# Transposes of a decoder layer moved from TensorE to VectorE and the GpSimd queue

## The chip, the cores and the metric

The kernel runs on one core of a Trainium2 chip. It is one program: one launch computes a whole decoder layer. The metric is the device time of one execution in microseconds (us).

## What is computed

One decoder layer on 256 tokens of width 2048 in float32, with a final RMS norm. The reference, cut to its skeleton:

```python
def parallel_mixer(h, w_in, ..., cos, sin, lam_init):
    z = h @ w_in
    qa, ka, va, qb, kb, vb, ga, gb = split_columns(z, IN_WIDTHS)
    qa, ka = partial_rope(qa, cos, sin), partial_rope(ka, cos, sin)
    oa = differential_attention(qa, ka, va, lam)      # 8 heads, two softmax maps each
    oa = rms_norm(oa, da_subln_g) * (1.0 - lam_init)  # per head, 128 values
    ob = stick_breaking_attention(qb, kb, vb)         # 8 heads, strictly causal
    merged = sigmoid(ga) * (oa @ w_proj_a) + sigmoid(gb) * (ob @ w_proj_b)
    return merged @ w_out

def reference(x, mem, ...):
    x = x + parallel_mixer(rms_norm(x, norm_mix_g), ...)
    x = x + memory_cross_attention(rms_norm(x, norm_x_g), rms_norm(mem, norm_mem_g), ...)
    x = x + conv_ffn(rms_norm(x, norm_ffn_g), ...)    # gated, causal convolution of width 3
    return rms_norm(x, final_norm_g)
```

## The kernel before

All weights stream from HBM in pieces of 1 MB, which the SyncE queue loads. `product` (L193) multiplies them: every piece is cut into two tiles of two 128-row blocks; ACT casts a tile to its high part (`whi`, L179), VectorE forms the low part (L180), and TensorE computes three matmuls for each block and token tile (high by high, high by low, low by high: L185 to L187). A tile costs TensorE 12 matmuls of 512 columns, a unit of 2048 rows by 512 columns costs 96. There are three buffers each for high and low parts, so a cast waits until the matmuls of the tile three before it are done. Sums stand in four PSUM buffers `mm`; a unit takes two, one for each half of the tokens, so a unit can start only when the sums of the unit two before it have been evicted.

The units run in this order: mixer queries, keys and values qa0, ka0, va0, qa1, ka1, va1 (differential attention) and qb0 to vb1 (stick-breaking), eight gates g12 to g19, four merge units (pa and pb, 8 blocks each, for n = 0 to 3), the output projection wo0 to wo3 with the first residual, then cross keys kx, queries qx and values vx, the cross output wxo, the up-projections and the down-projections.

Between the matmuls stands the other work. `product` calls `tick` after each tile; `spawn(generator, delay)` puts a piece of work on a list, and `tick` runs due pieces up to their next `yield`. That sets the order in which the code is written out. A scheduler then orders the instructions of each engine anew by its own timing model when the program is compiled, all but SyncE's; each engine executes its row in that fixed order.

An operand of a matmul needs its contraction axis on the partitions, so results have to be transposed:

- `proj_T` (L260) evicts a unit of queries or keys from PSUM by ACT (L266, scaled by the norm factor, into a buffer of the pool `wk`), rotates it on GpSimd where needed, and two ticks later transposes it by 8 TensorE transposes of 128 x 128 (L275) through PSUM and copies it out on VectorE (L277).
- `transposed` (L142) does the same in two halves (L151) and splits each into a high and a low part by ACT and VectorE (`split`, L117 and L118, or L122 and L123 with gains). Merge units (`mT`), both residuals (`x1T`, `x2T`) and the cross queries and keys (`proj_T2`, L251) use it.
- `turn` and `regroup` (L129, L138), which only the up-projection uses: VectorE transposes 32 x 32 blocks within a tile, and 16 transfers of 32 KB issued by GpSimd put the blocks into their places.

The pool `wk` has seven buffers of one kind (`w2`). They hold the evicted queries and keys before their transposition, and also the score maps, exponentials and outputs of the attention heads. A differential head (`diff_head`) is a chain: scores on TensorE (`sa`), mask, maxima, exponentials, scaling and combination on VectorE and ACT (`pa`), three transposes (`da_tp`), the product with the values (`oa`), a norm over 128 values whose power -0.5 GpSimd takes (L351), two transposes (`oaT`) and a split. Heads 0 to 3 are spawned after va0, heads 4 to 7 after va1. A stick-breaking pair (`sb`, `lb`, `cb`, `ab`, `ob`) is the like with scans. In the views, numbers of buffers are left out, so `qaT_z` is an evicted unit of queries.

Of the kernel before, what the change touches and what calls it, by code (L numbers as in the profile page):

```python
# [11 lines left out]
AF = mybir.ActivationFunctionType  # L12
ALU = mybir.AluOpType
# [3 lines left out]
P = 128  # L17
S = 256
# [27 lines left out]
def hybrid_layer(ctx: ExitStack, tc: tile.TileContext, x, xT, mem, memT, gmix, par, gfin,  # L46
# [16 lines left out]
    def col(name, i=None, n=1):  # L63
        if name == "g_mix":
            return gm[:, i:i + n]
        a, b = _PC[name]
        return pc[:, a:b] if i is None else pc[:, a + i:a + i + n]
# [21 lines left out]
    def spawn(gen, delay=0):  # L89
        tasks.append([clock[0] + delay, gen])  # L90
# [16 lines left out]
    def chunk_tile(name, shape):  # L107
        return b4.tile(shape, F32, tag="b4", name=name)

    def sm_tile(name):  # L110
        return ps_sm.tile([P, U], F32, tag="sm", name=name)
# [15 lines left out]
    def turn(blk, src, t):  # L127

        nc.vector.transpose(out=blk[:, :, t * P:(t + 1) * P], in_=src.rearrange("p (f c) -> p f c", c=P))  # L129
# [11 lines left out]
    def flip_tile(name):  # L141
        return chunk_tile(f"{name}_blk", [P, U // P, S])  # L142

    def transposed(dst, src, n, name, gains=None):

        for h in range(2):
            pt = sm_tile(f"{name}_tp").rearrange("p (j s) -> p j s", j=2)
            for j in range(2):
                for t in range(NT):
                    c = (2 * h + j) * P  # L150
                    nc.tensor.transpose(out=pt[:, j, t * P:(t + 1) * P],  # L151
                                        in_=src[:, t, c:c + P], identity=ident)
            k0 = 4 * n + 2 * h
            dst[k0 // 2] = act_tile(f"{name}_{h}")
            split(dst[k0 // 2], pt, None if gains is None else [gains(k0), gains(k0 + 1)])
        yield 0

    def sumsq(dst, src):
        junk = wk.tile([P, U], F32, tag="w2", name="junk")
        nc.scalar.activation(out=junk[:, :src.shape[-1]], in_=src, func=AF.Square, accum_out=dst)  # L160
# [87 lines left out]
                                op=ALU.mult)  # L248
        nc.gpsimd.tensor_tensor(out=v[:, :, 0:ROT], in0=a, in1=b, op=ALU.add)

    def proj_T2(ps, r, name):  # L251

        dst = [None, None]
        z = chunk_tile(f"{name}_z", [P, NT, U])
        for t in range(NT):
            nc.scalar.activation(out=z[:, t], in_=ps[t], func=AF.Copy, scale=r[:, t:t + 1])
        spawn(transposed(dst, z, 0, name), 2)
        return dst

    def proj_T(ps, r, name, rotate=False):  # L260

        dst = chunk_tile(name, [P, 4, S])
        zs = []
        for t in range(NT):
            z = wk.tile([P, U], F32, tag="w2", name=f"{name}_z")
            nc.scalar.activation(out=z, in_=ps[t], func=AF.Copy, scale=r[:, t:t + 1])  # L266
            if rotate:
                rope(z, t)
            zs.append(z)

        def rest():
            for t in range(NT):
                pt = sm_tile(f"{name}_tp")
                for h in range(4):
                    nc.tensor.transpose(out=pt[:, h * P:(h + 1) * P],  # L275
                                        in_=zs[t][:, h * P:(h + 1) * P], identity=ident)
                nc.vector.tensor_copy(out=dst[:, :, t * P:(t + 1) * P],  # L277
                                      in_=pt.rearrange("p (h s) -> p h s", h=4))
            yield 0
        spawn(rest(), 2)  # L280
        return dst

    def proj_n(ps, r, name):
# [20 lines left out]
    def diff_head(h):  # L304
# [43 lines left out]
        nc.vector.tensor_scalar(out=tot, in0=ss[:, :, 0], scalar1=1.0 / P, scalar2=EPS,  # L348
                                op0=ALU.mult, op1=ALU.add)
        ro = st.tile([P, NT], F32, tag="ro", name="ro")  # L350
        nc.gpsimd.tensor_tensor(out=ro, in0=tot, in1=mhalf[:, :NT], op=ALU.pow)  # L351
        o = wk.tile([P, NT, P], F32, tag="w2", name="o")
        for t in range(NT):
            nc.vector.tensor_scalar(out=o[:, t], in0=po[:, t], scalar1=ro[:, t:t + 1], scalar2=None,
# [120 lines left out]
    for n in range(4):  # L475
        ga, gb = gates[n], gates[4 + n]
        for g in (ga, gb):
            nc.scalar.activation(out=g, in_=g, func=AF.Sigmoid)
        pa = product(oaT, w_pa, n, 8, f"pa{n}")
        pb = product(obT, w_pb, n, 8, f"pb{n}")  # L480
        for t in range(NT):
            nc.vector.tensor_tensor(out=ga[:, t], in0=pa[t], in1=ga[:, t], op=ALU.mult)
            nc.vector.tensor_tensor(out=gb[:, t], in0=pb[t], in1=gb[:, t], op=ALU.mult)
            nc.gpsimd.tensor_tensor(out=ga[:, t], in0=ga[:, t], in1=gb[:, t], op=ALU.add)
        spawn(transposed(mT, ga, n, f"mT{n}"), 2)

    def residual(ps, base, n, ss):
        for t in range(NT):
# [18 lines left out]
    for n in range(4):  # L507
        xr.append(chunk_tile(f"xr{n}", [P, NT, U]))
        nc.sync.dma_start(out=xr[n], in_=x[n])
        ps = product(mT, w_out, n, KD, f"wo{n}")  # L510
        residual(ps, xr[n], n, ss1)
        spawn(transposed(x1T, xr[n], n, f"x1T{n}", lambda k: col("g_x", k)), 2)
        if n == 0:
            spawn(load_mem(), 0)
    r1 = scaled(rstd(ss1, NT, D, "r1"), 128 ** -0.5, "r1x")


    rm = rstd(rmss, NT, D, "rm")
    kx = proj_T2(product(memTt, w_xkv, 0, KD, "kx"), rm, "kxT")
    qx = proj_T2(product(x1T, w_xq, 0, KD, "qx"), r1, "qxT")  # L520
    oxT = [act_tile(f"oxT{i}") for i in range(2)]
    pT = [None] * 4

# [204 lines left out]
```

## Time and profile before

| | us |
|---|---|
| median of 3 runs (1500.5 to 1500.92) | 1500.87 |
| the profiled execution | 1501.38 |
| its span in the trace | 1499.6 |
| TensorE busy, share of the span | 1484.7, 99% |
| VectorE, ACT, GpSimd busy | 919.5, 781.6, 256.2 |

The profile is of one execution. Its lines are grouped by source line, engine and operation; "idle before" names what an engine waited for last. Matmuls overlap, and their ends are modelled, so prices of TensorE work are read from starts.

### The profile page before, as it was taken

The page shows a single profiled execution, that of the slowest core. Times are in us where ns is not written, and L with a number is a line of the kernel's source. Part 1 is how long each engine was busy: PE and PEld are TensorE (multiplying, and loading weights), DVE is VectorE, ACT ScalarE, POOL GpSimd, SP SyncE. Part 2 cuts the span into 40 slices and gives each one's busy share as a digit, 9 for nine tenths or more (in the row PEclk, how much of TensorE's full clock was granted, in tenths as well). Part 3 has the DMA queues.
Part 4 walks back from the last instruction along what each step waited for, and adds up shares of the span by engine and source line. Part 5 has one row for each costly group of instructions (what it writes and reads, how often), then busy time and mean ns, then how long its engine had stood idle before and what let it go on. Part 6 is the DMA issues. An engine that isn't in the chain of part 4 may idle for free.

```text
span 1499.6 us, 17849 instructions
## 1 busy us (share of the span) xinstructions
PE 1484.7 (99%) x6728; PEld 1225.4 (82%) x6728; DVE 919.5 (61%) x1175; ACT 781.6 (52%) x1074; POOL 256.2 (17%) x424
## 2 busy tenths in 40 slices
PE   8999999999999999999999999999999999999997
PEld 6878788888888888888888888888888888888886
DVE  5566666565444555665676677767777776644562
ACT  6454455456444444664565555556655655444441
POOL 0202000000000010000003344334434433000010
PEclk9999999999999999999999999999999999999999
DMA  9544444545555556765445666666676666655561
GB/s 346 188 150 169 160 149 169 171 168 194 191 189 189 189 201 212 274 233 177 166 163 194 228 218 219 218 220 225 197 234 217 216 208 223 221 197 196 199 231 75
DMA packets 55270, 299.35 MB, mean 200 GB/s; under 512 B 10640, under 2 KB 10640, under 8 KB 22416
## 3 DMA queue, kind: packets, MB, share of 16 engines
q1 hardware_dynamic: 43488, 286.13, 54.8%
q0 software_dynamic: 11264, 11.56, 3.0%
q8 instruction: 52, 0.85, 0.2%
q10 hardware_dynamic: 432, 0.53, 0.1%
q14 instruction: 34, 0.28, 0.1%
HBM read 284.54 MB, written 2.10 MB: 191 GB/s over the span
## 4 chain that ended last, share of the span: by engine, by line
PE 98%; issue 1%; DMA 1%; DVE 0%; ACT 0%; SPq 0%; POOLq 0%; POOL 0%; DVEq 0%
PE up_mm L185 11%; PE up_mm L187 11%; PE up_mm L186 11%; PE dn_mm L186 5%; PE dn_mm L187 5%; PE dn_mm L185 5%; PE g_mm L185 4%; PE g_mm L187 4%; PE g_mm L186 4%; PE wo_mm L187 2%; PE wo_mm L186 2%; PE wo_mm L185 2%; PE va_mm L186 1%; PE qb_mm L186 1%; PE qb_mm L185 1%; PE kb_mm L187 1%
## 5 line engine op out<-in xcount | busy, mean ns | idle before, releaser
L180 DVE TENSOR_TENSOR up_lo<-up_raw,up_hi 128x1024 fp32r<-128x1024 f32 x176 | 214.5, 1223 | 130.7 <-ACT up_hi L179 130.7
L179 ACT CAST up_hi<-up_raw 128x1024 fp32r<-128x1024 f32 x176 | 184.9, 1050 | 192.2 <-PE up_mm L187 176.0
L187 PE MATMUL up_mm<-up_hi,x2T 128*128 128x512 f32 x704 | 273.9, 389 | 0.0
L186 PE MATMUL up_mm<-up_lo,x2T 128*128 128x512 f32 x704 | 273.9, 389 | 0.0
L138 POOL DMA_DIRECT2D uT<-up_blk x352 | 202.5, 583 | 287.8 <-DVE up_blk L129 169.1
L185 PE MATMUL up_mm<-up_hi,x2T 128*128 128x512 f32 x704 | 246.1, 389 | 0.0
L180 DVE TENSOR_TENSOR dn_lo<-dn_raw,dn_hi 128x1024 fp32r<-128x1024 f32 x88 | 109.8, 1253 | 94.9 <-ACT dn_hi L179 89.8
L187 PEld LDWEIGHTS up_mm<-up_hi,x2T 128*128 128x128 f32 x704 | 132.1, 188 | 27.5
L185 PEld LDWEIGHTS up_mm<-up_hi,x2T 128*128 128x128 f32 x704 | 132.2, 188 | 27.3
L186 PEld LDWEIGHTS up_mm<-up_lo,x2T 128*128 128x128 f32 x704 | 132.1, 188 | 27.4
L179 ACT CAST dn_hi<-dn_raw 128x1024 fp32r<-128x1024 f32 x88 | 91.8, 1054 | 115.2 <-PE dn_mm L187 99.9
L186 PE MATMUL dn_mm<-dn_lo,gT 128*128 128x512 f32 x352 | 136.9, 389 | 0.0
L187 PE MATMUL dn_mm<-dn_hi,gT 128*128 128x512 f32 x352 | 136.9, 389 | 0.0
L180 DVE TENSOR_TENSOR g_lo<-g_raw,g_hi 128x1024 fp32r<-128x1024 f32 x64 | 78.4, 1225 | 83.9 <-ACT g_hi L179 83.9
L185 PE MATMUL dn_mm<-dn_hi,gT 128*128 128x512 f32 x352 | 125.9, 389 | 0.0
L179 ACT CAST g_hi<-g_raw 128x1024 fp32r<-128x1024 f32 x64 | 67.2, 1051 | 73.5 <-PE g_mm L187 70.3
L186 PE MATMUL g_mm<-g_lo,hT 128*128 128x512 f32 x256 | 100.0, 391 | 0.0
L187 PE MATMUL g_mm<-g_hi,hT 128*128 128x512 f32 x256 | 99.8, 390 | 0.0
L185 PE MATMUL g_mm<-g_hi,hT 128*128 128x512 f32 x256 | 90.7, 391 | 0.0
L185 PEld LDWEIGHTS dn_mm<-dn_hi,gT 128*128 128x128 f32 x352 | 66.1, 188 | 13.8
L186 PEld LDWEIGHTS dn_mm<-dn_lo,gT 128*128 128x128 f32 x352 | 66.1, 188 | 13.8
L187 PEld LDWEIGHTS dn_mm<-dn_hi,gT 128*128 128x128 f32 x352 | 66.0, 188 | 13.6
(301 smaller groups left out, 2702.8 us busy)
## 6 DMA issues: line engine op xcount, KB each, us to landing
up_raw<-in_w_up SPq DMA_DIRECT2D x88, 1024.0 KB, 5.2
dn_raw<-in_w_dn SPq DMA_DIRECT2D x44, 1024.0 KB, 4.9
g_raw<-in_w_in SPq DMA_DIRECT2D x32, 1024.0 KB, 4.8
wo_raw<-in_w_out SPq DMA_DIRECT2D x16, 1024.0 KB, 4.9
uT<-up_blk POOLq DMA_DIRECT2D x352, 32.0 KB, 3.8
ka_raw<-in_w_in SPq DMA_DIRECT2D x8, 1024.0 KB, 6.3
va_raw<-in_w_in SPq DMA_DIRECT2D x8, 1024.0 KB, 4.8
qb_raw<-in_w_in SPq DMA_DIRECT2D x8, 1024.0 KB, 4.8
```

The costliest lines, as they stand in the source:

```text
L138: nc.gpsimd.dma_start(out=d[b * q:(b + 1) * q, :, a * q:(a + 1) * q], in_=s[a * q:(a + 1) * q, :, b * q:(b + 1) * q])
L179: nc.scalar.copy(out=hi, in_=src)
L180: nc.vector.tensor_tensor(out=lo, in0=src, in1=hi.bitcast(F32), op=ALU.subtract)
L185: nc.tensor.matmul(out, lhsT=a[0], rhs=b[0], start=start, stop=False)
L186: nc.tensor.matmul(out, lhsT=a[0], rhs=b[1], start=False, stop=False)
L187: nc.tensor.matmul(out, lhsT=a[1], rhs=b[0], start=False, stop=stop)
```

## The change

A new helper `flipped` takes the place of `transposed` for merge units 0 to 2, for all four units of the first residual and for the cross keys: two turns on VectorE, 16 transfers on the GpSimd queue into a tile `z`, a pause of seven ticks, and two splits from `z`. Merge unit 3, the cross queries and the second residual keep `transposed`. `proj_T` turns and regroups straight into its destination, one tick after the eviction in place of two. In the head norm the power moves from GpSimd to ACT as exp(-0.5 ln(x)), with four VectorE steps that refine it.

```diff
+    def flipped(dst, src, n, name, gains=None):
+
+        blk = flip_tile(name)
+        for t in range(NT):
+            turn(blk, src[:, t], t)
+        z = chunk_tile(f"{name}_z", [P, U // P, S])
+        regroup(z, blk)
+        yield 7
+        for h in range(2):
+            k0 = 4 * n + 2 * h
+            dst[k0 // 2] = act_tile(f"{name}_{h}")
+            split(dst[k0 // 2], z[:, 2 * h:2 * h + 2], None if gains is None else [gains(k0), gains(k0 + 1)])
+        yield 0
...
-    def proj_T2(ps, r, name):
+    def proj_T2(ps, r, name, how, delay):
...
-        spawn(transposed(dst, z, 0, name), 2)
+        spawn(how(dst, z, 0, name), delay)
...
         def rest():
+            blk = flip_tile(name)
             for t in range(NT):
-                pt = sm_tile(f"{name}_tp")
-                for h in range(4):
-                    nc.tensor.transpose(out=pt[:, h * P:(h + 1) * P],
-                                        in_=zs[t][:, h * P:(h + 1) * P], identity=ident)
-                nc.vector.tensor_copy(out=dst[:, :, t * P:(t + 1) * P],
-                                      in_=pt.rearrange("p (h s) -> p h s", h=4))
+                turn(blk, zs[t], t)
+            regroup(dst, blk)
             yield 0
-        spawn(rest(), 2)
+        spawn(rest(), 1)
...
-        nc.gpsimd.tensor_tensor(out=ro, in0=tot, in1=mhalf[:, :NT], op=ALU.pow)
+
+        nc.scalar.activation(out=ro, in_=tot, func=AF.Ln)
+        nc.scalar.activation(out=ro, in_=ro, func=AF.Exp, scale=-0.5)
+        nc.vector.tensor_tensor(out=tot, in0=tot, in1=ro, op=ALU.mult)
+        nc.vector.tensor_tensor(out=tot, in0=tot, in1=ro, op=ALU.mult)
+        nc.vector.tensor_scalar(out=tot, in0=tot, scalar1=-0.5, scalar2=1.5, op0=ALU.mult, op1=ALU.add)
+        nc.vector.tensor_tensor(out=ro, in0=ro, in1=tot, op=ALU.mult)
...
-        spawn(transposed(mT, ga, n, f"mT{n}"), 2)
+        spawn((transposed if n == 3 else flipped)(mT, ga, n, f"mT{n}"), 2 if n == 3 else 1)
...
-        spawn(transposed(x1T, xr[n], n, f"x1T{n}", lambda k: col("g_x", k)), 2)
+        spawn(flipped(x1T, xr[n], n, f"x1T{n}", lambda k: col("g_x", k)), 1)
...
-    kx = proj_T2(product(memTt, w_xkv, 0, KD, "kx"), rm, "kxT")
-    qx = proj_T2(product(x1T, w_xq, 0, KD, "qx"), r1, "qxT")
+    kx = proj_T2(product(memTt, w_xkv, 0, KD, "kx"), rm, "kxT", flipped, 1)
+    qx = proj_T2(product(x1T, w_xq, 0, KD, "qx"), r1, "qxT", transposed, 2)
```

The change also moves instructions when the program is compiled. Three places follow; a row has the source line, the operation, what is written and read, the size and a count of equal rows.

First TensorE in unit kb0 and at its end, where differential heads 5 to 7 run (`sa` scores, `da_tp` transposes of weights, `oa` output, `oaT` its transposes). Before, in the middle of kb0:

```order
L186 MATMUL kb_mm_1686<-kb_lo,hT_216 128x512
L187 MATMUL kb_mm_1686<-kb_hi,hT_216 128x512
L185 MATMUL kb_mm_1685<-kb_hi,hT_216 128x512
L341 MATMUL oa<-va_1380,da_aT 128x128
L342 MATMUL oa<-va_1380,da_aT 128x128
L343 MATMUL oa<-va_1380,da_aT 128x128
L294 MATMUL da_tp<-ident,pa_1667 128x128
L295 MATMUL da_tp<-ident,pa_1667 128x128
L296 MATMUL da_tp<-ident,pa_1667 128x128
L186 MATMUL kb_mm_1685<-kb_lo,hT_216 128x512
L187 MATMUL kb_mm_1685<-kb_hi,hT_216 128x512
L185 MATMUL kb_mm_1686<-kb_hi,hT_216 128x512
```

Now, behind kb0's last matmul, with vb0's first as the last row:

```order
L376 MATMUL oaT<-ident,o 128x128 x2
L323 MATMUL sa_1712<-kaT_1254,qaT_1015 128x128
L323 MATMUL sa_1712<-kaT_1254,qaT_1015 128x256
L323 MATMUL sa_1713<-kaT_1254,qaT_1015 128x128
L323 MATMUL sa_1713<-kaT_1254,qaT_1015 128x256
L305 MATMUL da_tp<-ident,pa_1678 128x128
L306 MATMUL da_tp<-ident,pa_1678 128x128
L307 MATMUL da_tp<-ident,pa_1678 128x128
L352 MATMUL oa<-va_1428,da_aT 128x128
L353 MATMUL oa<-va_1428,da_aT 128x128
L354 MATMUL oa<-va_1428,da_aT 128x128
L199 MATMUL vb_mm_1970<-vb_hi,hT_109 128x512
```

One head's output and the next head's weights stood among kb matmuls; now the heads' steps stand in a block with no unit's matmul among them, up to vb0's first. The ACT row there has the eviction of qb0 behind the exponentials of the second of these heads.

Second ACT between merge unit 3 (`pb_hi` is the cast of its weights) and the output projection (`wo_hi`); the casts `mT` are splits of transposed merge units. Before:

```order
L117 CAST mT_0_4354<-mT_tp 128x512
L117 CAST mT_1_4362<-mT_tp 128x512
L179 CAST pb_hi<-pb_raw 128x1024 x3
L179 CAST wo_hi<-wo_raw 128x1024 x5
L117 CAST mT_0_4520<-mT_tp 128x512
L117 CAST mT_1_4528<-mT_tp 128x512
L179 CAST wo_hi<-wo_raw 128x1024 x2
L122 ACTIVATE memT_4663<-memT_raw_4661,pc 128x256
```

Now:

```order
L117 CAST mT_1_4418<-mT_z 128x512
L193 CAST pb_hi<-pb_raw 128x1024 x4
L117 CAST mT_0_4589<-mT_z 128x512
L117 CAST mT_1_4592<-mT_z 128x512
L117 CAST mT_0_4646<-mT_tp 128x512
L117 CAST mT_1_4654<-mT_tp 128x512
L193 CAST wo_hi<-wo_raw 128x1024 x10
```

The splits of merge units 2 and 3 moved ahead of the first wo cast; the last one before it needs merge unit 3's result. On TensorE the eight transposes of merge unit 3 moved from the third tile of wo0 to between pb3's last and wo0's first matmul.

Third ACT in gate units 13 to 15, where stick-breaking pairs 2 and 3 run (`lb` and `ab` are exponentials and logarithms, L478 or L495 is a gate's sigmoid). Before:

```order
L287 ACTIVATE gate_2823<-g_mm_2603,r_489 128x512
L287 ACTIVATE gate_2823<-g_mm_2604,r_489 128x512
L388 ACTIVATE lb<-lb 128x512
L179 CAST g_hi<-g_raw 128x1024
L478 ACT_TABLE_LOAD
L478 ACTIVATE gate_2823<-gate_2823 128x1024
L179 CAST g_hi<-g_raw 128x1024
L400 ACT_TABLE_LOAD
L400 ACTIVATE ab<-cb 128x512
L179 CAST g_hi<-g_raw 128x1024 x3
L117 CAST obT_2881<-ob 128x512
```

Now:

```order
L193 CAST g_hi<-g_raw 128x1024
L495 ACT_TABLE_LOAD
L495 ACTIVATE gate_2919<-gate_2919 128x1024
L404 ACT_TABLE_LOAD
L404 ACTIVATE lb<-lb 128x2x128
L193 CAST g_hi<-g_raw 128x1024
L405 ACT_TABLE_LOAD
L405 ACTIVATE lb<-lb 128x2x128
L193 CAST g_hi<-g_raw 128x1024
L417 ACT_TABLE_LOAD
L417 ACTIVATE ab<-cb 128x2x128
L403 ACTIVATE lb<-sb 128x512
```

The sigmoid of gate 12 moved from behind a pair's logarithm to between its first two steps, and the loads of activation tables between it and the pairs' steps went from three in this stretch to seven.

## Rows read from the trace of the kernel before

**Rows 1.** The page, engines' busy time and TensorE's granted clock in 40 slices:

```profile
PE 1484.7 (99%) x6728; PEld 1225.4 (82%) x6728; DVE 919.5 (61%) x1175; ACT 781.6 (52%) x1074; POOL 256.2 (17%) x424
...
PEclk9999999999999999999999999999999999999999
```

**Rows 2.** TensorE's waits: engine, line, producer; us in all, times, longest:

```profile
PE qa_mm L185 <- ACT qa_hi L179: 6.0, 1, 6.0
PE qa_mm L186 <- DVE qa_lo L180: 0.4, 1, 0.4
```

**Rows 3.** Timeline of TensorE: start, us, engine, line, operation, count, around x1T's transposes:

```profile
608.37 0.39 PE L186 MATMUL wo_mm<-wo_lo,mT 128*128 128x512 f32 x1
608.60 0.39 PE L187 MATMUL wo_mm<-wo_hi,mT 128*128 128x512 f32 x1
608.83 1.03 PE L151 MATMUL x1T_tp<-ident,xr 128*128 128x128 f32 x8
609.62 0.48 PE L185 MATMUL wo_mm<-wo_hi,mT 128*128 128x512 f32 x1
609.94 0.40 PE L186 MATMUL wo_mm<-wo_lo,mT 128*128 128x512 f32 x1
```

**Rows 4.** Lines of GpSimd (busy, mean ns), and page: issue size, us to landing:

```profile
L138 POOL DMA_DIRECT2D uT<-up_blk x352 | 202.5, 583 | 287.8 <-DVE up_blk L129 169.1 <-DVE u L587 71.5 <-issue 31.0
...
uT<-up_blk POOLq DMA_DIRECT2D x352, 32.0 KB, 3.8
```

**Rows 5.** Timeline of ACT and VectorE around diff head 3:

```profile
109.66 0.74 DVE L332 SCALAR_TENSOR_TENSOR pa<-pa,sm,pa 128x128 f32<-128x128 f32 x2
...
111.49 0.48 DVE L365 SCALAR_TENSOR_TENSOR oaT<-oaT,gsub,oaT 128x256 fp32r<-128x256 f32 x1
...
111.88 0.75 DVE L315 TENSOR_TENSOR sa<-sa,mask_le 128x256 f32<-128x256 f32 x2
...
112.54 1.14 DVE L318 TENSOR_REDUCE nm<-sa 128x1 f32<-128x128 f32 x4
...
114.24 0.36 ACT L324 ACTIVATE pa<-sa,nm 128x128 f32<-128x128 f32 x1
...
115.83 1.27 ACT L266 ACTIVATE qaT_z<-qa_mm,r0a 128x512 f32<-128x512 f32 x2
...
115.98 0.18 DVE L326 RECIPROCAL sm<-sm 128x4 f32<-128x4 f32 x1
...
116.33 0.54 DVE L330 TENSOR_SCALAR pa<-pa,sm 128x128 f32<-128x128 f32 x2
```

**Rows 6.** Lines by form of ACT and VectorE, 60 to 330 us:

```profile
L179 ACT CAST kb_hi<-kb_raw 128x1024 fp32r<-128x1024 f32 x16 | 16.8, 1052 | 18.5 <-PE kb_mm L187 10.7 <-PE qb_mm L187 6.6 <-issue 1.1
...
L266 ACT ACTIVATE kbT_z<-kb_mm,r 128x512 f32<-128x512 f32 x4 | 2.7, 689 | 2.4 <-PE kb_mm L187 2.4
...
L180 DVE TENSOR_TENSOR kb_lo<-kb_raw,kb_hi 128x1024 fp32r<-128x1024 f32 x16 | 19.6, 1223 | 12.5 <-ACT kb_hi L179 12.5
```

**Rows 7.** The same view, stick-breaking pairs:

```profile
L387 ACT ACTIVATE lb<-lb 128x512 f32<-128x512 f32 x3 | 1.9, 633 | 0.1
...
L394 DVE TENSOR_TENSOR_SCAN cb<-ones,lb 128x256 f32<-128x256 f32 x6 | 3.8, 679 | 0.1
```

**Rows 8.** Timeline of TensorE and GpSimd at the end of merge unit 3:

```profile
580.66 0.61 PE L185 MATMUL wo_mm<-wo_hi,mT 128*128 128x512 f32 x2
...
581.19 3.53 POOL L484 TENSOR_TENSOR gate<-gate,gate 128x512 f32<-128x512 f32 x2 [19.19 <-issue]
```

**Rows 9.** Lines by form of ACT, 480 to 600 us:

```profile
L117 ACT CAST mT<-mT_tp 128x512 fp32r<-128x512 f32 x8 | 4.3, 590 | 4.5 <-PE mT_tp L151 4.5
```

**Rows 10.** Lines by form of ACT, whole span: loads of activation tables:

```profile
L478 ACT ACT_TABLE_LOAD x2 | 2.6, 1283 | 0.0
```

**Rows 11.** Timeline of TensorE in the first microseconds:

```profile
9.60 0.63 PE L186 MATMUL qa_mm<-qa_lo,hT 128*128 128x512 f32 x1
10.03 0.63 PE L187 MATMUL qa_mm<-qa_hi,hT 128*128 128x512 f32 x1
```

## The prediction

> **What bounds the kernel now.** I read the page first. TensorE is busy 99% of the span at the full granted clock [rows 1]. Then I read what TensorE waits for: 6.0 and 0.4 us in the first microseconds and nothing after that [rows 2]. Whatever shortens the row of instructions on TensorE shortens the kernel; whatever makes TensorE wait once lengthens it, for there is no idle time that could take a wait up. So I price two things only: the TensorE instructions that go, and the places where the new order makes TensorE wait. The profiled run took 1501.38 us, 0.51 above the median of 1500.87; I sum against it and take 0.5 off.
>
> **What is removed.** Sixteen groups of eight transposes leave TensorE: 3 of merge units, 4 of the residual, 1 of the cross keys, 8 of queries and keys. The stretch with one such group shows its price. Matmuls start 0.23 apart; between the last before the group (608.60) and the first after it (609.62) lie 1.02, and the next start comes 0.32 later instead of 0.23 [rows 3]: 1.02 - 0.23 + 0.09 = 0.88 us, and where the group is cut in two the dearer following start comes twice, so about 0.92. 16 x 0.92 = 14.7 us. From the eight starts alone (0.79) it would be 12.7.
>
> The Trainium skill ("TensorE: Matmul & The Clock Gate", Part 4: PE-mode transpose) gives about 275 ns for a transpose in a kernel; by that figure the 128 would be worth 35 us and the sum below would end near 1506. The 0.79 for eight above disagrees with it, and the measured spacing decides.
>
> **What is added beside other work.** Per unit VectorE turns two tiles in place of two copies from PSUM, of about the same length, and the GpSimd queue issues 16 transfers at 583 ns, 9.3 us, which land 3.8 us after issue [rows 4]. The turning and the transfers themselves are off TensorE. But a key that was ready one copy after its transposes now waits for two turns, 9.3 of issue and 3.8 of landing, some 14 us, so the attention heads start later, and the compiled order shows where they now stand: at unit boundaries.
>
> **Second boundary of heads (kb0 to vb0): +9.5 us.** In the first extract on the change, TensorE had one head's steps spread between kb matmuls; now 20-odd small ones stand in a block behind kb0's last matmul, and vb's first matmul waits for the eviction of qb0, which stands on ACT behind all exponentials of the last head (they hold the buffers it needs). From the start of kb0's last matmul, at 0: it ends at 0.4; a cast for vb that waits for it ends at 1.45 and its low part on VectorE at about 2.75 [rows 6]. Behind that stand two masks (0.75), an output step (0.48) and four maxima (1.14): 5.1. Norm steps and exponentials (114.24 to the eviction at 115.83, so 1.6) run side by side to 6.4. Reciprocal to scalings (115.98 to 116.87) 0.9, output step 0.48, first mask 0.4, combination 0.74: 8.9. The other head's maxima and mask 1.5, its last two exponentials 0.8, the eviction 0.69: 12.0 [rows 5, 6]. Off that go 0.2 of the usual spacing and some 21 small matmuls of 0.11 (eight took 0.79) that run inside it: 9.5.
>
> **First boundary of heads (ka1 to va1): +6.5.** The same chain, with one head's scores already up before ka1's last ten matmuls. From 0: cast to 1.45, four exponentials to 3.05, low part and masks beside them, then maxima, scalings and combination of both heads on VectorE to about 6.5, two more exponentials 0.8 and the eviction 0.69 to 7.9; less 0.2 and nine small matmuls: 6.5 to 6.9 [rows 5, 6].
>
> **Pair boundary (kb1 to vb1): +7.5.** Two casts and the first score block run to 2.4; then, each behind the other, three ACT steps on 512 columns (3 x 0.63), on VectorE two scans of 0.68 and a step of like length on either side, an exponential of 0.63, the eviction 0.69: 2.4 + 1.9 + 2.7 + 1.3 = 8.3; less 0.2 and six transposes: 7.5 [rows 5, 7].
>
> **Merge to output projection (pb3 to wo0): +7.0.** This unit keeps its transposes, but they moved from the third tile of wo0 to a place ahead of its first matmul, and on ACT the split of mT3 now stands ahead of the first wo cast (second extract). From wo's start in the trace, 580.66, as 0: GpSimd's two additions end at 4.06 [rows 8]; the last six transposes end at about 4.8; two casts of mT 0.59 each to 6.0 [rows 9]; the wo cast 1.05 to 7.1; its low part 1.22 to 8.3 [rows 6]. Third matmul at 8.3 instead of 0.45, with the eight transposes (0.9) inside: 7.0.
>
> **Gates (g12 to g15): +2.5.** The sigmoid of gate 12 now stands between exponentials of pair 2 (third extract): four more table loads of 1.28 [rows 10] fall between casts that have about 3.1 us of slack (two tiles of 12 matmuls at 0.227, 5.44, less 1.05 and 1.22). Summed step by step the low parts come 0.7, 0.1 and 1.1 late, and g15's first matmul waits 1.2 behind a cast and an eviction; some stands under pair work. Bounds 1 to 4.
>
> **Cross attention (vx to wxo): +2.5.** The cross keys land later, so the last head's softmax stands behind vx's last matmul. I have no row for exactly this wait; one head's exponentials plus scalings (0.8 + 1.0) are the lower bound, 3.5 with casts between them the upper.
>
> **Small edits at nothing.** The head norm's power leaves GpSimd for two short ACT and four short VectorE steps; their place in the chains above is counted. Merge units 0 to 2 and x1T have a unit's length (96 matmuls, 21.8 us) for about 19 us of gate additions, turns, issue and landing [rows 4, 8], so nothing waits for them; if that cover failed, qx or wo would wait the few microseconds over.
>
> **Clock: +4.8.** After the 6.0 us without a matmul at the start, the first matmuls start 0.43 apart, not 0.23 [rows 11, 3], about 12 of them: 2.4 us lost. That is the spacing of 1.2 GHz in place of 2.4 GHz, although the granted clock reads full in this slice too [rows 1]. Four of the waits (heads twice, pair, merge) are 6.5 us or more with only small matmuls in them. The trace has no such wait in mid-kernel; the later gap of 0.4 cost no slow matmuls. Bounds 0 and 4 x 2.4 = 9.6; I take the middle.
>
> The Trainium skill ("TensorE: Matmul & The Clock Gate", the table under Why this matters for your kernels) says that an idle gap of TensorE between bursts of matmuls sends it back to the half clock; by that the whole 9.6 is paid. The start agrees; for mid-kernel no run here shows it.
>
> **Sum.** 9.5 + 6.5 + 7.5 + 7.0 + 2.5 + 2.5 = 35.5 of waiting; + 4.8 of clock; - 14.7. That is + 25.6: 1501.4 + 25.6 - 0.5 = **1526.5**, say 1526.
>
> **Rivals.** (a) *The full clock price at all four waits*: + 4.8 more, 1531; with chains a fifth longer as well, 1538. For it speaks the start of this kernel; against it, that transposes and score matmuls stand inside each wait. (b) *Clock never falls*: 1521.5. Both belong to the same mechanism as the forecast. (c) *Half-hidden waits*: the vector chains overlap more than my sums of single durations (in rows 5 four maxima take 1.14 where their step apart would be longer), the six waits come to 18 and the clock stays: 1501.4 + 3.3 - 0.5 = 1504. (d) *Not slower: the score blocks at the boundaries find their operands ready*. If casts for the next unit, the masks and the exponentials end about when the block is reached, as they do for the head in rows 5, only the transposes' 14.7 is left: 1486. It decides from the point where the six waits sum to less than 14.7, that is 2.4 each instead of 5.9. For it speaks that the up stage already uses the turn and the transfers with no wait of TensorE [rows 2, 4]; against it, that vb's cast, the masks, the exponentials and the eviction are queued one behind the other after the last matmul, which no slack before that matmul shortens. (e) *The change does not do what it says*: a key could land after its head's place; at least a unit of 21.8 us lies between a key's eviction and its first scores in the new order, against some 14, so I give it nothing of its own.
>
> **How the numbers follow.** Forecast with (b): 0.62; (a): 0.2; (c): 0.1; (d): 0.08. From 1503 (the low end of (c)) to 1541 (full clock, waits a quarter longer: 44 + 9.6 - 14.7) lie eight in ten. What a measurement of this kernel can tell from no change is 0.2%, 3 us: faster than 1498 has (d) and a rest, 0.09; within 3 us the lower half of (c), 0.06; slower 0.85.
>
> **What would show it.** In the new profile TensorE's waits must list, behind the start, va and vb for ACT evictions of qaT_z and qbT_z, sa and da_tp for VectorE, mT_tp for GpSimd's gate additions and wo for ACT or VectorE, of several microseconds each; TensorE's busy share must fall to 97 or 98%; matmuls behind each wait must start 0.43 apart where the clock fell. If these waits are under a microsecond, the step of the boundary chains is wrong. If they are there but the time is near 1504, my sums were too long.

## The result, and the profile after

The changed kernel takes 1526.31 us (median of four runs, 1525.39 to 1526.96) against 1500.89 for the kernel before: a ratio of 1.0169, 95% interval 1.0156 to 1.0181. The forecast was 1526. The profiled execution took 1526.9, its span 1525.1.

The page of the changed kernel, busy time of the engines and TensorE's granted clock in 40 slices, as in [rows 1]:

```profile
PE 1481.5 (97%) x6600; PEld 1220.1 (80%) x6600; DVE 934.8 (61%) x1223; ACT 788.4 (52%) x1094; POOL 395.0 (26%) x672
...
PEclk9999989999999999999999999999999999999999
```

TensorE has 128 instructions fewer, the transposes. Its busy time fell by 3.2 us, and the span outside it rose from 14.9 (1499.6 - 1484.7) to 43.6 us: 28.7 us of new idle time. TensorE's waits say where (columns as in [rows 2]; the largest eleven rows):

```profile
PE qa_mm L199 <- ACT qa_hi L193: 6.5, 2, 5.7
PE sb_tp L306 <- ACT ab L417: 4.8, 1, 4.8
PE oaT L376 <- DVE o L371: 4.7, 2, 3.8
PE da_tp L305 <- DVE pa L343: 3.8, 2, 2.9
PE sxT L561 <- DVE pa L555: 3.1, 1, 3.1
PE mT_tp L151 <- POOL gate L501: 2.7, 2, 1.5
PE wo_mm L199 <- ACT wo_hi L193: 2.0, 2, 1.8
PE sb_tp L305 <- ACT ab L417: 1.7, 1, 1.7
PE wo_mm L200 <- DVE wo_lo L194: 1.3, 2, 0.8
PE oa L352 <- DVE da_aT L309: 1.3, 1, 1.3
PE g_mm L199 <- ACT gate L298: 1.0, 1, 1.0
```

The first row is the start. The heads (`da_tp`, `oaT`, `oa`), a pair (`sb_tp`), the gates (`g`), the last merge unit (`mT_tp`, then `wo`) and the cross attention (`sxT`) are where the forecast put them. The instructions that wait are in part others than it named as its sign: it wanted several microseconds before `va` and `vb` for evictions and before `sa`, but `va` waited 0.5 us for one, and `vb` and `sa` have no row. The waits stand earlier in the same chains, before `oaT`, `da_tp` and `sb_tp`.

The stages, each from the first matmul of its first unit to the first of the next stage, in the profiled executions (the up and down stages are alike in all kernels, 719.3 us):

```
                  mixer       gates   pa0..pb2   pb3    kx     vx
                  ka0..vb1    g12-19  and pa3    + wo   + qx   + wxo
before            279.6       179.7   79.0       101.6  45.3   55.3
after             292.6       183.7   76.2       109.5  43.5   60.9
difference        +13.0       +4.0    -2.8       +7.9   -1.8   +5.6
by the forecast   +19.7       +2.5    -2.8       +5.4   -1.8   +2.5
```

(The forecast's terms sorted into stages: 9.5 + 6.5 + 7.5, three quarters of the clock's 4.8, less eight groups at 0.92, for the mixer; 7.0 and a quarter of the 4.8, less three groups of `x1T`, for pb3 and wo.) The measured row sums to 25.8 before rounding, of which 0.3 come back in a shorter start; the forecast's sums to 25.5.

The longest block, between kb0 and vb0, on TensorE (start, us, count, in brackets the idle time before and its releaser):

```profile
204.63 0.39 PE L201 MATMUL kb_mm<-kb_hi,hT 128*128 128x512 f32 x1
...
210.62 0.66 PE L376 MATMUL oaT<-ident,o 128*128 128x128 f32 x2 [3.85 <-DVE o L371]
...
216.02 0.79 PE L352 MATMUL oa<-va,da_aT 128*128 128x128 f32 x2 [1.31 <-DVE da_aT L309]
217.32 0.77 PE L199 MATMUL vb_mm<-vb_hi,hT 128*128 128x512 f32 x1
217.89 0.63 PE L200 MATMUL vb_mm<-vb_lo,hT 128*128 128x512 f32 x1
218.32 0.63 PE L201 MATMUL vb_mm<-vb_hi,hT 128*128 128x512 f32 x1
```

From kb0's last matmul to vb0's first are 12.69 us (forecast 12.0); 35 small instructions stand between. On ACT the eviction of qb0 runs from 216.34, and vb0's first matmul follows it. The next two start 0.43 apart, the spacing of [rows 11], not the 0.23 of [rows 3]. Stretches in the waits and behind them (us, then busy time and count of TensorE, weight loads, VectorE, ACT, GpSimd, then the granted clock, DMA share, GB/s):

```profile
131.00:134.00 3.00, 3.00 (x7) 2.34 (x8) 2.44 (x6) 0.39 (x1) 2.77 (x8) 0.50 0.00 0
205.00:209.00 4.00, 1.77 (x17) 1.20 (x15) 2.86 (x8) 2.35 (x8) 0.00 (x0) 1.00 0.76 262
210.50:217.00 6.50, 4.22 (x17) 2.76 (x18) 5.10 (x18) 3.13 (x13) 0.00 (x0) 0.50 0.00 0
217.00:220.00 3.00, 3.00 (x10) 2.45 (x9) 2.46 (x9) 1.64 (x8) 0.46 (x1) 0.50 0.00 0
299.00:302.00 3.00, 3.00 (x8) 2.32 (x8) 2.79 (x6) 1.07 (x2) 1.10 (x2) 0.50 0.00 0
601.00:605.00 4.00, 3.96 (x10) 2.67 (x9) 2.90 (x3) 1.26 (x2) 0.00 (x0) 0.50 0.30 68
767.00:770.00 3.00, 3.00 (x8) 2.38 (x8) 0.00 (x0) 0.00 (x0) 0.00 (x0) 0.50 0.02 5
```

Behind each of the four waits the granted clock is 0.50, that is 1.2 GHz, while TensorE is busy nearly throughout. In the longest block it has fallen before the block ends, so its last 19 small instructions run at 0.50 too. The last row is a fifth fall, behind the wait in the cross attention.

### The profile page after: what moved, and what is told of

Its sections match the earlier page's. It is cut to its first block, busy times and chain, and to the rows that moved or that the text cites. A ratio compares the mean times of both kernels' runs of the same rounds, so it can differ in the third digit from the quotient of the medians.

```text
span 1525.1 us, 18033 instructions
## 1 busy us (share of the span) xinstructions
PE 1481.5 (97%) x6600; PEld 1220.1 (80%) x6600; DVE 934.8 (61%) x1223; ACT 788.4 (52%) x1094; POOL 395.0 (26%) x672
## 4 chain that ended last, share of the span: by engine, by line
PE 58%; DMA 1%; issue 1%; DVE 0%; ACT 0%; POOL 0%; POOLq 0%; DVEq 0%; ACTq 0%
PE up_mm L201 10%; PE up_mm L199 10%; PE up_mm L200 10%; PE dn_mm L200 5%; PE dn_mm L199 5%; PE dn_mm L201 5%; PE wo_mm L200 2%; PE wo_mm L201 1%; PE wo_mm L199 1%; DMA x1T_z<-x1T_blk 1%; PE wxo_mm L199 0%; PE wxo_mm L200 0%; PE vx_mm L201 0%; PE vx_mm L199 0%; PE vx_mm L200 0%
```

## The experiments

The theory: the loss is the sum of chains that now stand between two units, plus slow matmuls behind them, and each part of the change carries its own share. The rivals are named with each run. Ratios are against the kernel before, with 95% intervals. Each diff is against the changed kernel unless said otherwise.

**Queries and keys back on TensorE.**

```diff
-            blk = flip_tile(name)
             for t in range(NT):
-                turn(blk, zs[t], t)
-            regroup(dst, blk)
+                pt = sm_tile(f"{name}_tp")
+                for h in range(4):
+                    nc.tensor.transpose(out=pt[:, h * P:(h + 1) * P],
+                                        in_=zs[t][:, h * P:(h + 1) * P], identity=ident)
+                nc.vector.tensor_copy(out=dst[:, :, t * P:(t + 1) * P],
+                                      in_=pt.rearrange("p (h s) -> p h s", h=4))
             yield 0
-        spawn(rest(), 1)
+        spawn(rest(), 2)
```

> The changed kernel with the transposes of mixer queries and keys back on TensorE; merge units 0 to 2, residual, cross keys and head norm stay changed. Theory (waits at named places): the three blocks of head steps at unit ends go, and the gate units lose their extra waits. Mixer and gate stages cost 13.0 + 4.0 more than before in the changed kernel, so 1526.3 - 17 = about 1509; the wait at the merge's end and in the cross stage stay. Rival (the cost is spread over all the new transfers and turns, 25.4 us for 16 groups): 8 groups fewer, 1526.3 - 12.7 = 1513.6, with the mixer's waits only thinned.

1510.84 us, ratio 1.0069 (1.0052 to 1.0086). The mixer takes 278.7 us (before 279.6), the gates 179.7, as before: both losses belong to queries and keys. The rest of the change keeps some 10 us of loss: the waits of this kernel are the merge (2.7 us), the `wo` casts (3.6) and the cross attention (3.1).

**Queries and keys alone**, in the kernel before (diff against it; the power of the head norm stays on GpSimd there):

```diff
+            blk = flip_tile(name)
             for t in range(NT):
-                pt = sm_tile(f"{name}_tp")
...
+                turn(blk, zs[t], t)
+            regroup(dst, blk)
             yield 0
-        spawn(rest(), 2)
+        spawn(rest(), 1)
```

> The kernel before with only the mixer queries and keys turned on VectorE and regrouped by transfers. Theory (waits at named places): head steps in blocks at unit ends, so 1500.9 + 17 = about 1518, a little more if the head norm's power on GpSimd makes the blocks' chains longer; no wait at the merge's end or in the cross stage. Rival (spread over the transfers): 8 groups, 1500.9 + 12.7 = 1513.6.

1521.56 us, ratio 1.0139 (1.0124 to 1.0154): more than either expected. The gates take 183.7 and the merge, `wo` and cross stages are those of before, but the mixer takes 297.3 us, 4.7 more than in the changed kernel. The part left out, the power on ACT, had to be the reason; the next run tests it.

**The power back on GpSimd.**

```diff
-        nc.scalar.activation(out=ro, in_=tot, func=AF.Ln)
-        nc.scalar.activation(out=ro, in_=ro, func=AF.Exp, scale=-0.5)
...
-        nc.vector.tensor_tensor(out=ro, in0=ro, in1=tot, op=ALU.mult)
+        nc.gpsimd.tensor_tensor(out=ro, in0=tot, in1=mhalf[:, :NT], op=ALU.pow)
```

> The changed kernel with the head norm's power back on GpSimd, everything else as changed. Theory: GpSimd issues the transfers of queries and keys in the same stretch, so a power of 0.7 us that stands behind 16 issues (9.3 us) makes the heads' chains longer; the run with only queries and keys turned, which had it on GpSimd, was 3.6 above the sum of the stages: 1526.3 + 3.6 = about 1530. Rival (the power's place is hidden): 1526, or up to 1 us less for fewer VectorE and ACT steps.

1533.43 us, ratio 1.0218 (1.0204 to 1.0232), 7 us slower than the changed kernel, more than the 3.6 expected. On GpSimd (start, us) the power of one head stands behind 16 issues in a row:

```profile
133.53 9.24 POOL L138 DMA_DIRECT2D qaT<-qaT_blk  x16 [1.05 <-DVE qaT_blk L129]
142.79 0.72 POOL L363 TENSOR_TENSOR ro<-st_o,mhalf 128x2 f32<-128x2 f32 x1
```

TensorE's waits for the head's output `o` come to 8.1 us in three waits instead of 4.7 in two, and the mixer takes 297.9 us, 5.3 more than in the changed kernel:

```profile
PE oaT L371 <- DVE o L366: 8.1, 3, 2.7
```

So the power on ACT gains several us here, and it does so because the transfers fill the GpSimd queue: with queries and keys on TensorE, as in the first experiment, the mixer gains 0.9 from it.

**Evicted queries and keys in buffers of their own.** Is a block long because the key comes late, or because the eviction needs a buffer of `wk` that the heads still hold?

```diff
         zs = []
+        zz = chunk_tile(f"{name}_zz", [P, NT, U])
         for t in range(NT):
-            z = wk.tile([P, U], F32, tag="w2", name=f"{name}_z")
+            z = zz[:, t]
```

> The changed kernel with evicted mixer queries and keys in a buffer of their own instead of two of the seven that the head steps also use. Theory A (the eviction that waits for the heads' buffers is what holds up va and vb): va1, vb0 and vb1 no longer wait for it, heads may stand between their matmuls, the blocks' waits shrink by half or more (21.8 to 10 or less): 1526.3 - 10 = about 1515. Theory B (the heads stand at unit ends because their keys land late, the buffers matter little): 1524 to 1527.

1511.06 us, ratio 1.0067 (1.0051 to 1.0083). The mixer falls from 292.6 to 274.0 us, 5.6 below the kernel before, and the clock does not fall in it. Around the same place as above, the small steps are followed by vb0 with no wait:

```profile
211.28 0.38 PE L377 MATMUL oaT<-ident,o 128*128 128x128 f32 x2
211.59 0.93 PE L324 MATMUL sa<-kaT,qaT 64*128 64x128 f32 x8
212.45 0.73 PE L199 MATMUL vb_mm<-vb_hi,hT 128*128 128x512 f32 x2
```

The long blocks are gone; five waits of up to 1.7 us for the evictions remain:

```profile
PE vb_mm L199 <- ACT qbT_zz L281: 2.2, 2, 1.4
PE qb_mm L199 <- ACT kaT_zz L281: 1.7, 1, 1.7
```

The late key by itself costs little: what made the blocks was that an eviction, and with it the next unit, had to come behind a whole head for want of a buffer. The new buffers come from another pool, so the heads also have the seven of `wk` to themselves, and the compiled order changes with it; the run shows that the blocks hang on the shared pool, not which of the two undoes them. The gates do not gain from it; they take 185.4 us, and pb3 with wo takes 112.4.

**One more merge group back on TensorE.**

```diff
-        spawn((transposed if n == 3 else flipped)(mT, ga, n, f"mT{n}"), 2 if n == 3 else 1)
+        spawn((transposed if n >= 2 else flipped)(mT, ga, n, f"mT{n}"), 2 if n >= 2 else 1)
```

> The changed kernel with merge unit 2 transposed on TensorE again, like unit 3. In the compiled order the transposes of unit 3 then stand in wo0 again and the wo casts ahead of its split. Theory: the wait between merge and output projection, 9.2 with the slow matmuls behind it, goes, one group of 0.96 comes back: 1518. Rival (spread over the transfers): one group of 16 fewer, 1524.7.

1519.66 us, ratio 1.0126 (1.0111 to 1.0141). pb3 and wo take 101.1 us instead of 109.5, the merge units 0.9 more. So the wait hangs on the group of mT2. In the changed kernel, on TensorE:

```profile
594.20 0.39 PE L201 MATMUL pb_mm<-pb_hi,obT 128*128 128x512 f32 x1
596.10 0.44 PE L151 MATMUL mT_tp<-ident,gate 128*128 128x128 f32 x2 [1.52 <-POOL gate L501]
...
600.43 1.22 PE L199 MATMUL wo_mm<-wo_hi,mT 128*128 128x512 f32 x2 [1.78 <-ACT wo_hi L193]
601.69 0.80 PE L200 MATMUL wo_mm<-wo_lo,mT 128*128 128x512 f32 x1
```

And there on ACT, on GpSimd and on VectorE:

```profile
594.75 1.14 ACT L117 CAST mT<-mT_z 128x512 fp32r<-128x512 f32 x2 [7.23 <-DMA mT_z<-mT_blk]
```

```profile
594.78 2.94 POOL L501 TENSOR_TENSOR gate<-gate,gate 128x512 f32<-128x512 f32 x2 [4.51 <-DVE gate L500]
```

```profile
595.40 2.87 DVE L118 TENSOR_TENSOR mT<-mT_z,mT 128x512 fp32r<-128x512 f32 x2
```

ACT's row has mT2's split ahead of mT3's and of the first `wo` cast, and ACT stands 7.23 us until mT2's transfers have landed. mT2's low parts (`mT_z`) run on VectorE while GpSimd makes the sums for mT3, and mT3's own split and the `wo` cast come behind. With mT2 on TensorE the compiled order is another: two `wo` casts run before the merge ends, and mT3's transposes stand in wo0 again. The run does not part mT2's late data from that order.

**Ten matmuls more in that wait.** Does the matmul spacing behind the wait come from TensorE having had little to do? Ten extra matmuls on a copy by ACT, whose result nobody reads, are put into the wait; the rest stays.

```diff
+        if n == 3:
+            gd = wk.tile([P, U], F32R, tag="w2", name="gd")
+            nc.scalar.copy(out=gd, in_=pb[0])
+            dm = sm_tile("dm")
+            for i in range(10):
+                nc.tensor.matmul(dm, lhsT=gd[:, 0:P], rhs=gd, start=True, stop=True)
```

> The changed kernel with work added that nobody needs: when merge unit 3's first sum is there, ACT copies it once more (0.7 us) and TensorE multiplies the copy ten times by itself (10 x 0.23 = 2.3 us), in the wait ahead of the transposes of unit 3. The output is not touched by it. Theory (the clock falls in the wait): TensorE is less idle there, the first wo matmuls start 0.23 apart instead of 0.43 and the granted clock of that stretch reads above the 0.50 of the changed kernel; 2 us or so less than the changed kernel, 1524. Rival (the first wo matmuls are slow because their casts come late): spacing stays 0.43, and time is the same or up to 0.7 more, 1526 to 1527.

1525.38 us, ratio 1.0161 (1.0147 to 1.0176); the interval overlaps that of the changed kernel, so the time alone decides nothing. The trace does, on TensorE:

```profile
594.22 2.56 PE L507 MATMUL dm<-gd 128*128 128x512 f32 x10 [0.72 <-ACT gd L504]
...
600.70 0.51 PE L200 MATMUL wo_mm<-wo_lo,mT 128*128 128x512 f32 x1 [0.53 <-DVE wo_lo L194]
```

And the stretch that answers to the last one of the changed kernel above:

```profile
601.00:605.00 4.00, 4.00 (x19) 3.27 (x18) 2.52 (x3) 1.33 (x2) 0.00 (x0) 1.00 0.56 172
```

The granted clock stays at 1.00 here, 2.4 GHz, and matmuls start 0.23 apart; pb3 and wo together take 2.6 us less although ten matmuls more stand in them (106.9; the changed kernel and the four others with the same merge units and x1T take 109.1 to 112.4). The wait for `wo_hi` is the same 1.78 us. So the slow matmuls are tied to how little TensorE did before them, not to the step that is waited for.

**Cross keys back, and x1T back**, one at a time:

```diff
-    kx = proj_T2(product(memTt, w_xkv, 0, KD, "kx"), rm, "kxT", flipped, 1)
+    kx = proj_T2(product(memTt, w_xkv, 0, KD, "kx"), rm, "kxT", transposed, 2)
```

> The changed kernel with the cross keys transposed on TensorE again. Theory: the waits of the cross stage (5.65 more than before in the changed kernel) go, a group of 0.89 comes back: 1521.5. Rival (spread over the transfers): 1524.7.

```diff
-        spawn(flipped(x1T, xr[n], n, f"x1T{n}", lambda k: col("g_x", k)), 1)
+        spawn(transposed(x1T, xr[n], n, f"x1T{n}", lambda k: col("g_x", k)), 2)
```

> The changed kernel with the first residual's four units transposed on TensorE again. Theory (waits at named places): the waits of 1.5 us in wo that stand behind late splits go, four groups of 0.92 come back: 1526.3 - 1.5 + 3.7 = 1528.5, slower. Rival (spread over the transfers): four groups of 16 fewer, 1526.3 - 6.4 = 1519.9, faster.

1520.68 us (1.0135, 1.012 to 1.015) and 1520.77 us (1.0131, 1.0117 to 1.0146). The second contradicts the theory: it foresaw that transposes would come back and nothing else change but 1.5 us of waits. The number is near the rival's 1519.9, but the gain is not spread as the rival has it. In both kernels vx and wxo take 55.3 us, as before, and the wait of `sxT` is gone. So that wait needs both parts at once. GpSimd's issues for the cross keys, in the changed kernel and then without x1T on its queue:

```profile
721.83 8.75 POOL L138 DMA_DIRECT2D kxT_z<-kxT_blk  x15 [10.21 <-DVE x1T L123]
```

```profile
715.70 7.51 POOL L138 DMA_DIRECT2D kxT_z<-kxT_blk  x13 [20.54 <-issue]
```

With x1T on the queue they start 14.7 us ahead of vx's first matmul (736.56), without it 19.5 ahead (735.23): 4.8 us later. GpSimd stood idle before both, so a full queue is not the reason. The turn of the keys on VectorE is; in the changed kernel and then without x1T's turns:

```profile
719.95 1.30 DVE L129 STREAM_TRANSPOSE kxT_blk<-kxT_z 128x512 f32<-128x512 f32 x2
```

```profile
713.77 1.33 DVE L129 STREAM_TRANSPOSE kxT_blk<-kxT_z 128x512 f32<-128x512 f32 x2 [0.51 <-ACT kxT_z L270]
```

The keys are evicted 22.2 us ahead of vx in both kernels, but turned 16.6 ahead in one and 21.5 in the other: these are the same 4.8 us. In the changed kernel two more low parts of `qx` stand ahead of the turn in VectorE's row. And no gain is seen from x1T's three groups in the `wo` units: pb3 and wo take 109.6 us with their transposes and 109.5 without.

**Three kernels without the parts that lost.** First: queries, keys (as in the first experiment), mT2 and cross keys on TensorE; mT0, mT1, x1T and the power as in the change.

```diff
-        spawn((transposed if n == 3 else flipped)(mT, ga, n, f"mT{n}"), 2 if n == 3 else 1)
+        spawn((transposed if n >= 2 else flipped)(mT, ga, n, f"mT{n}"), 2 if n >= 2 else 1)
...
-    kx = proj_T2(product(memTt, w_xkv, 0, KD, "kx"), rm, "kxT", flipped, 1)
+    kx = proj_T2(product(memTt, w_xkv, 0, KD, "kx"), rm, "kxT", transposed, 2)
```

> Only the parts that my reading says pay: merge units 0 and 1 and the first residual turned on VectorE, head norm power on ACT; queries and keys, merge units 2 and 3 and the cross keys transposed on TensorE. Theory (waits at named places): 1500.9 - 2 x 0.96 - 4 x 0.92 + 1.5 = 1496.8, faster than both kernels. Rival (cost spread over the transfers, 1.6 for each group): six groups, 1500.9 + 9.5 = 1510.

1498.58 us, ratio 0.9981 (0.9972 to 0.999): 0.2% faster than before, and 1.8 us above the expected time. One wait is left, 2.1 us in the first residual; behind it the granted clock is 0.50 for some 3 us.

Second: the same with x1T on TensorE, and the cross keys as in the change (only the line of x1T is shown).

```diff
-        spawn(flipped(x1T, xr[n], n, f"x1T{n}", lambda k: col("g_x", k)), 1)
+        spawn(transposed(x1T, xr[n], n, f"x1T{n}", lambda k: col("g_x", k)), 2)
```

> Merge units 0 and 1 and the cross keys turned on VectorE, head norm power on ACT, all else transposed on TensorE. From the stage sums: mixer 1.0 less (as in the run without turned queries and keys), merges 1.92 less, cross queries 0.89 less, residual as before, and with the residual's transfers gone the cross keys' transfers start on time, so no wait in the cross stage: 1500.9 - 3.8 = 1497.1. If the cross keys' transfers are late by themselves, 5.6 more, 1502.7.

1497.04 us, ratio 0.9975 (0.9965 to 0.9985). TensorE waits in its first microseconds alone, as in the kernel before. So the 2.1 us of the first were x1T's: pb3 and wo take 101.5 us here and took 102.8 there, so turning x1T loses 1.3 us although three groups of transposes are gone.

Third: the second, with qa and ka (those with `rotate`) by VectorE and transfers too, and all evicted queries and keys in buffers of their own.

```diff
+        zz = chunk_tile(f"{name}_zz", [P, NT, U])
...
+            z = zz[:, t]
...
+            if not rotate:
+                for t in range(NT):
+                    pt = sm_tile(f"{name}_tp")
...
+            else:
+                blk = flip_tile(name)
...
+        spawn(rest(), 1 if rotate else 2)
```

> Evicted queries and keys in a buffer of their own; differential queries and keys (the rotated ones), merge units 0 and 1 and the cross keys turned on VectorE; stick-breaking queries and keys, merge units 2 and 3 and the residual transposed on TensorE; head norm power on ACT. From the stage sums of the runs so far: the first half of the mixer 6.1 less than before, as in the run with own buffers, the second half as before, merges 2 x 0.96 less, cross queries 0.89 less: 1500.9 - 8.9 = 1492, if the gate stage loses its extra table loads. If own buffers moved the head steps only from one boundary to the next, 1498 or more.

1496.78 us, ratio 0.9972 (0.9961 to 0.9983); its interval overlaps the second's, and it lies between the two times expected. The mixer is 3.5 us shorter than in the second (275.2 against 278.7), and the gates give 2.9 back (182.6 against 179.7). Both beat the kernel before by about 4 us.

## Why the prediction came out

**Step that held: TensorE is the bound, and only removed instructions and new waits count.** Idle time rose by 28.7 us, in the places named. The second of the last three kernels, in which no wait was added, has three groups of transposes fewer: 3 x 0.92 = 2.8, and its mixer is 0.9 shorter with the power on ACT, 3.7 in all; it gained 3.8 against the 1500.84 of the kernel before in the same series.

**Transposes: right.** A merge unit falls from 11.84 to 10.88 us, 0.96; kx and qx together 1.8 for two groups. The Trainium skill's figure for a transpose ("TensorE: Matmul & The Clock Gate", Part 4: PE-mode transpose, about 275 ns) would have been 2.2 us for a group; the runs disagree with it.

**Boundaries: the chains right.** Last matmul to first of the next unit, with the forecast of the same stretch: kb0 to vb0 12.69 (12.0), ka1 to va1 7.62 (7.9), kb1 to vb1 8.13 (8.3). Summing single durations behind the last cast and eviction gave each within 0.7, in part by luck: the ends of these blocks ran at half clock, which the sums did not have (eight score matmuls took 1.66 us behind the fall in the longest block and 0.93 ahead of it). The condition that the forecast named, evictions that stand behind exponentials because the heads hold their buffers, is the cause: buffers of their own removed the blocks. But it acts through the order and not as a wait of its own, for `vb` never waits for an eviction.

**Mixer as a whole: wrong by 6.7, the other way.** The forecast took 7.4 for eight groups of transposes and 4.1 for small matmuls inside the blocks, 11.5 in all, as the work that leaves the spaces between the unit's matmuls. By the starts, before the change 54 groups of small instructions (276 in all) cost 38.9 us there; after it 21 groups outside the blocks (150) cost 19.2. So 19.7 left, 8 more than counted. Eight score matmuls of a pair, 1.3, went from vb1 into the gates. The blocks took in 54 small instructions where the forecast had counted 36, which is 2.0 at its own price. The rest, about 5, goes to that price, 0.11, taken from eight transposes in a row, and this is the step that failed. Score matmuls between large ones are dearer, as one place of the kernel before shows: from 68.66 to 70.06 are 1.40, less two starts of 0.23 is 0.95 for four of them, against 0.44 by that price.

```profile
68.66 0.61 PE L185 MATMUL va_mm<-va_hi,hT 128*128 128x512 f32 x2
69.21 0.92 PE L312 MATMUL sa<-kaT,qaT 64*128 64x128 f32 x4
70.06 0.50 PE L186 MATMUL va_mm<-va_lo,hT 128*128 128x512 f32 x1
```

With the blocks' 0.2 over and the clock's 1.6 (below), this makes 6.4 of the 6.7. It is read from the traces alone; no run isolates it, and small instructions that stayed but were grouped anew are in the 5.

**Clock: half of it missed.** The forecast took half the price of four falls. It fell at all four; in order of time 8, 7, 9 and about 10 slow matmuls lost about 1.7, 1.6, 1.9 and 2.5, 7.7 us instead of 4.8. A fifth fall, in the cross attention, was not in the forecast. So the Trainium skill's rule ("TensorE: Matmul & The Clock Gate", Why this matters for your kernels: an idle gap between bursts of matmuls returns the clock to half) holds here for gaps that small matmuls interrupt, and rival (a) had the better mechanism on this point. The forecast read the granted clock as full at the start [rows 1]. That reading does not hold: the trace has no record of this clock before 11.58 us, and the page counts such time as full.

**Merge to output projection: 5.9 for 7.0.** The two additions took 2.94, not 3.53, and the third `wo` matmul came at 601.69. The stage still lost 2.5 more than the forecast, 10.7 (7.9 and the 2.8 of x1T's groups) for 8.2: 5.9 + 2.5 of clock + 1.5 of the waits in the next paragraph are 9.9; 0.8 is not told apart.

**x1T at no cost: wrong.** Waits of 0.2, 0.5 and 0.8 us stand in the `wo` units, and 2.1 in the first of the three last kernels. GpSimd stops within a group, by the profile for its own transfers, and the transfers land 5.4 us after issue, not the 3.8 of [rows 4]. ACT then waits for x1T's data with the `wo` casts queued behind that split. GpSimd's timeline in the changed kernel:

```profile
628.15 4.60 POOL L138 DMA_DIRECT2D x1T_z<-x1T_blk  x8 [30.43 <-issue]
...
638.86 1.16 POOL L138 DMA_DIRECT2D x1T_z<-x1T_blk  x2 [2.33 <-DMA x1T_z<-x1T_blk]
```

The issues, with their size and the time to landing:

```profile
x1T_z<-x1T_blk POOLq DMA_DIRECT2D x64, 32.0 KB, 5.4
```

And ACT:

```profile
644.77 1.71 ACT L122 ACTIVATE x1T<-x1T_z,pc 128x256 fp32r<-128x256 f32 x4 [4.57 <-DMA x1T_z<-x1T_blk]
```

The step that failed is that a unit's length covers some 19 us of steps, "so nothing waits for them": it asked whether the data is there by the unit's end, not what is queued behind the split that waits for it. It failed for mT2 in the same way, where ACT stood 7.23 us.

**Cross attention: 5.6 for 2.5.** A wait of 3.06 and one of 0.4 are seen, and behind the first the clock fell: 12 matmuls of the output `ox` start 0.36 us apart, where 16 started 0.20 apart before, which is 1.8 us. After the change, then before it:

```profile
766.64 0.30 PE L561 MATMUL sxT<-ident,pa 128*128 128x128 f32 x1 [3.06 <-DVE pa L555]
766.78 4.44 PE L575 MATMUL ox<-pT,vx 128*128 128x256 f32 x12
```

```profile
744.01 3.62 PE L558 MATMUL ox<-pT,vx 128*128 128x256 f32 x16
```

The price lay within bounds of 1.8 to 3.5, which had no clock in them; and its cause, a turn of the keys that VectorE starts 4.8 us later when it turns x1T too, was no term of the forecast. **Gates: 4.0 for 2.5**, at the upper end of their bounds of 1 to 4: the waits of 0.8 and 1.0 cost 2.2 with the dear starts behind them, the eight score matmuls that came from vb1 cost 1.4 and were no term, and 0.4 is not told apart.

In sum, the forecast was too high by 6.7 in the mixer and too low by 2.5, 1.5 and 3.1 in the stages behind. Its closeness to a microsecond is the sum of these, and so luck; the sign and the 20 to 30 us rest on the chains, which did hold. Rivals (c) and (d) fell with the waits: no boundary was under the 2.4 us that (d) needed. Two of its sums are off by a little, and nothing hangs on them: (b) comes to 1521.7 and the upper end of the range to 1540.

**Open.** Whether the ten extra matmuls are worth their 2.6 us in the time itself. Which step of the compiled order puts the keys' turn late when x1T is turned too. And why the kernels in which the clock falls scatter by 1 to 4 us, where the kernel before and the last two, in which it does not fall between their start and end, scatter by about 1.

## What to carry to other kernels

Where TensorE never waits, take a transpose off it only where its result is wanted much later, and look at what is queued ahead of the turn and behind each step that now waits for the transfers: on VectorE, on the issuing queue, on the engine that splits the result, and in the pool that holds the source. Before a result is delayed, give the evictions that share its pool buffers of their own; here that turned a loss of 13 us in the mixer into a gain of 5.6. Price small matmuls at the place where they stand, since the same one costs more between large matmuls than in a row or in a wait.

## What the runs showed of the hardware

A wait with some small matmuls in it is enough for the clock to fall: the granted clock read 1.00 during the wait at 205 to 209 (17 TensorE instructions, 1.77 us busy of 4.00) and 0.50 from 210.5 on, after an idle time of 3.85 us. Ten matmuls of 512 columns in the merge's wait kept it at 1.00.

VectorE's low part of a 128x512 tile from SBUF took 1.43 us (2.87 for two) while GpSimd was adding, and 0.65 (1.29 for two) for the cross keys, also from SBUF, with GpSimd at rest:

```profile
741.71 1.29 DVE L118 TENSOR_TENSOR kxT<-kxT_z,kxT 128x512 fp32r<-128x512 f32 x2
```

The Trainium skill ("SBUF — State Buffer", Who interferes with whom) says that a VectorE instruction with two SBUF inputs contends with GpSimd instructions that read SBUF; the trace agrees.
